# Three 256-column matmuls per weight block become one of 512 and one of 256 columns, with the PSUM halves added afterwards

## The chip, the cores and the metric

The kernel runs on one core of one Trainium2 chip. The metric is the device time of one execution in microseconds (us), as the median of several executions.

## What is computed

Two transformer layers are applied to one sequence of 256 tokens with a width of 2048, all in float32. The first layer mixes tokens with a causal multi-scale pooling and an RWKV-7 recurrence, then has a squared-ReLU feed-forward part and a gated embedding. The second mixes with gated linear attention (GLA) and a sparse attention (NSA), then has a SiLU-gated feed-forward part. The change touches only how some dense products are computed. Cut to those:

```python
z = rms_norm(x, attn_norm) @ w_in
h2 = rms_norm(x, mlp_norm)
x = x + jnp.square(jax.nn.relu(h2 @ w_ffn_up)) @ w_ffn_down
...
proj = n @ w_in_2
f = silu(m @ w_gate) * (m @ w_up)
x = x + f @ w_down
```

## The kernel before, in words

TensorE has a fast float32 mode (`F32R` in the code) that rounds its operands. To keep float32 accuracy the kernel splits each operand into a high part, rounded to that mode, and a low part, the remainder, and adds three products: high times high, high times low, low times high. The activations are split once, by `split` (lines 247 to 249): ScalarE copies the value to the rounded high part, VectorE subtracts it to get the low part. The weights are split as they arrive: `stream` (lines 236 to 245) takes a 128x1024 block of raw weights that a DMA has loaded, ScalarE writes its high part `h` (line 240), VectorE its low part `l` (line 244; in the first mixer one block in eight goes to GpSimd).

There are two kinds of dense product.

- `gemm_a` (lines 251 to 266) makes one output tile with 128 output features on the partitions and 256 tokens on the columns. A piece of the weight, 128x128, is the stationary operand and the activation, 128x256, is the moving one. A tile runs over 16 such pieces (two raw blocks of eight) with three matmuls each (lines 262 to 264), and all 48 add into the same 256 columns of PSUM. `first_tiles` (lines 363 to 376) does the same for three tiles at once at the start of each layer (lines 373 to 375).
- `gemm_b_part` (lines 729 to 744) has the activation as the stationary operand and 512 columns of weights as the moving one (lines 740 to 742). The change leaves it as it is.

`gemm_a` and `first_tiles` together make 216 tiles: 35 in the first layer's mixer (24 of them in `rwkv_front`, 8 in `pool_path`, 3 in `first_tiles`), 64 in its feed-forward part (`w_ffn_up`, line 838), 29 in the second mixer, and 88 in the second feed-forward part (`ffn2`, lines 1343 and 1346). With 16 pieces each that is 3456 pieces.

Results leave PSUM from the pool `acc`, four banks of 128x512. One VectorE multiplication by the row scale takes a tile out in most places (lines 352, 640, 922, 939, 1188, 1343, 1346); in the first feed-forward part it is a ReLU on ScalarE (line 840), and VectorE then squares the result (line 842). In `rwkv_front` and `pool_path` two tiles share one bank, 256 columns each (lines 423 to 425 and 633 to 635). Throughout the recurrence one of the four banks is held by `rwkv_post`.

The order of the instructions on each engine comes from a scheduler in the language's tile layer, which lays out the whole program by its own estimates; each engine then runs its queue in that order. A change of one instruction's length can therefore move others.

Of the kernel before, what the change touches and what calls it, by code (L numbers as in the profile page):

```python
# [19 lines left out]
T = 256  # L20
# [148 lines left out]
class Kern:  # L169
# [81 lines left out]
    def gemm_a(self, w, i, act, o=None):  # L251
        nc = self.nc
        if o is None:
            o = self.acc.tile([128, 512], F32, name="acc", tag="acc")[:, :T]
        n = len(act)
        k = 0
        for half in range(n // 8):
            h, l = self.stream(w[i, half].rearrange("p k n -> p (k n)"))
# [7 lines left out]
        return o  # L266

    def act_pair(self):
        return [self.big.tile([128, 16, T], F32R, name="x" + p, tag="x" + p) for p in "hl"]

    def act_tiles(self):
        return [[x[:, k] for k in range(16)] for x in self.act_pair()]

    def quart_tile(self, part, dtype=F32):
        return self.quart.tile([128, 4, T], dtype, name="q" + part, tag="q" + part)

    def half_tiles(self, parts=2):
        out = [], []
        for _ in range(parts):
            for side, part in zip(out, "hl"):  # L280
                q = self.quart_tile(part, F32R)
                side += [q[:, k] for k in range(4)]
        return out
# [18 lines left out]
    def block1_in(self):  # L302
        nc, I = self.nc, self.I
        xh, xl = self.act_tiles()
# [10 lines left out]
        for q in range(4):  # L315
            r = self.quart_tile("h")
            raws.append(r)
# [3 lines left out]
            for k in range(4):  # L321
                g = self.p("attn_norm", q * 4 + k)
                nc.scalar.activation(xh[q * 4 + k], r[:, k], AF.Copy, scale=g)
                nc.vector.scalar_tensor_tensor(xl[q * 4 + k], r[:, k], g, xh[q * 4 + k].bitcast(F32), ALU.mult, ALU.subtract)
        self.raws = raws
        return list(zip(xh, xl))

    def block1_stats(self):
# [3 lines left out]
        for q, r in enumerate(self.raws):  # L332
            sq = self.quart_tile("l")
# [13 lines left out]
    def shifted(self, pool, ps, mu, tag, out=None, bufs=2):  # L347
# [4 lines left out]
        nc.vector.tensor_mul(z[:, 1:], ps, self.rb)  # L352
# [10 lines left out]
    def first_tiles(self, w, n, act):  # L363
        nc = self.nc
        out = [self.acc.tile([128, 512], F32, name="acc", tag="acc")[:, :T] for _ in range(n)]
        for half in range(2):
            for i in range(n):
                h, l = self.stream(w[i, half].rearrange("p k n -> p (k n)"))
                for q in range(8):
                    k = half * 8 + q  # L370
                    wh, wl = h[:, q * 128:(q + 1) * 128], l[:, q * 128:(q + 1) * 128]
                    xh, xl = act[k]
                    nc.tensor.matmul(out[i], wh, xh, start=k == 0, stop=False)
                    nc.tensor.matmul(out[i], wh, xl, start=False, stop=False)
                    nc.tensor.matmul(out[i], wl, xh, start=False, stop=k == 15)  # L375
# [22 lines left out]
    def rwkv_front(self, j, act):  # L398
# [8 lines left out]
        if j in (3, 4):  # L407
            x = self.quart_tile("h").rearrange("p k t -> p (k t)")
            AR = x[:, :512].rearrange("p (c x t) -> p c x t", c=4, x=2)
            BKt = x[:, 512:].rearrange("p (c t) -> p c t", c=4)  # L410
            G = self.quart_tile("l").rearrange("p k t -> p (k t)").rearrange("p (h c t) -> p h c t", h=2, c=4)
# [4 lines left out]
        if j == 3:  # L416
            x = self.quart_tile("l").rearrange("p k t -> p (k t)")
# [962 lines left out]
```

## Time and profile before

| | us |
|---|---|
| median of 3 runs | 2485.6 (2485.5 to 2490.12) |
| profiled execution, first to last instruction (its span; the page gives no other time for it) | 2485.7 |
| TensorE matmul busy | 2455.0 (99%) |
| TensorE weight load busy | 2224.1 (89%) |
| VectorE busy | 1547.7 (62%) |
| ScalarE busy | 1149.9 (46%) |
| GpSimd busy | 217.5 (9%) |

In the profile PE is TensorE's matmuls, PEld its weight loads, DVE is VectorE, ACT is ScalarE, POOL is GpSimd. Matmuls are pipelined: a record lasts from a matmul's start until its last result is written, and the next starts long before that. So the busy time of PE only says whether there was a matmul under way; what a matmul costs is the distance from its start to the start of the next.

The stages, by the places of their lines in the trace: the first mixer until about 375 us, its output projection until about 450 us, the first feed-forward part until about 1150 us, the gated embedding until about 1297 us, the second mixer and its projection until about 1720 us, the second feed-forward part until the end.

### The profile page before, as it was taken

To read this page: it belongs to the slowest core of one execution; us is meant where nothing else is said; L and a number is where in the kernel's file an instruction comes from. 1 tells how busy PE (TensorE), PEld (TensorE's weight loads), DVE (VectorE), ACT (ScalarE), POOL (GpSimd) and SP (SyncE) were. 2 spreads that over 40 slices of the span, in tenths; PEclk is the share of its full clock that TensorE was granted. 3 is DMA by queue.
4 is the path that set the end of the run, shared out by engine and by line. 5 is a ranking of instruction groups with operands and counts; after the bars stand their busy time and mean duration, and the time that the engine had idled before them with its cause. 6 is when DMAs were issued, how large, how long until landed. Compare 5 with 4: busy or idle time off the path is not lost.

```text
span 2485.7 us, 40916 instructions
## 1 busy us (share of the span) xinstructions
PE 2455.0 (99%) x16396; PEld 2224.1 (89%) x16396; DVE 1547.7 (62%) x2436; ACT 1149.9 (46%) x1686; POOL 217.5 (9%) x321
## 2 busy tenths in 40 slices
PE   9999999999999999999999998999999999999999
PEld 8988888989989989988887897888989999998988
DVE  7788866555555555556674677766555555555555
ACT  5545445544444444445652466545444444444443
POOL 1543320000000000000010044200000000000000
PEclk9999999999999999999999999999999999999999
DMA  6443336555555555556556543255555655555554
GB/s 230 153 130 111 97 115 237 182 192 186 187 190 185 188 192 187 187 189 235 180 184 213 179 149 118 90 196 185 179 190 185 187 186 186 188 185 187 186 190 158
DMA packets 135406, 439.59 MB, mean 177 GB/s; under 512 B 26784, under 2 KB 29216, under 8 KB 134064
## 3 DMA queue, kind: packets, MB, share of 16 engines
q1 hardware_dynamic: 130032, 423.58, 52.1%
q10 hardware_dynamic: 5184, 13.41, 1.4%
q8 instruction: 128, 2.10, 0.3%
q14 instruction: 62, 0.51, 0.1%
HBM read 429.59 MB, written 7.34 MB: 176 GB/s over the span
## 4 chain that ended last, share of the span: by engine, by line
PE 94%; DVE 4%; ACT 1%; DMA 1%; issue 1%; POOL 0%; SPq 0%; DVEq 0%; ACTq 0%
PE acc L262 16%; PE acc L263 16%; PE acc L264 16%; PE acc L740 13%; PE acc L741 13%; PE acc L742 13%; PE ch L361 3%; PE fr L361 2%; DVE l L244 1%; PE fr L782 1%; PE acc L361 1%; PE ch L582 0%; PE ch L585 0%; DVE X L1002 0%; PE acc L375 0%
## 5 line engine op out<-in xcount | busy, mean ns | idle before, releaser
L244 DVE TENSOR_TENSOR l<-r,h 128x1024 fp32r<-128x1024 f32 x774 | 951.5, 1230 | 737.0 <-ACT h L240 728.8
L240 ACT CAST h<-r 128x1024 fp32r<-128x1024 f32 x780 | 818.8, 1050 | 1102.2 <-PE acc L742 448.1
L262 PE MATMUL acc<-qh,h 128*128 128x256 f32 x1824 | 520.8, 286 | 0.0
L264 PE MATMUL acc<-qh,l 128*128 128x256 f32 x1824 | 519.3, 285 | 0.0
L263 PE MATMUL acc<-ql,h 128*128 128x256 f32 x1824 | 519.2, 285 | 0.0
L264 PE MATMUL acc<-xh,l 128*128 128x256 f32 x1536 | 439.0, 286 | 0.5 <-DVE l L244 0.5
L262 PE MATMUL acc<-xh,h 128*128 128x256 f32 x1536 | 439.4, 286 | 0.0
L263 PE MATMUL acc<-xl,h 128*128 128x256 f32 x1536 | 438.6, 286 | 0.0
L262 PEld LDWEIGHTS acc<-qh,h 128*128 128x128 f32 x1824 | 350.5, 192 | 4.0 <-issue 3.5
L263 PEld LDWEIGHTS acc<-ql,h 128*128 128x128 f32 x1824 | 350.5, 192 | 1.7 <-issue 1.2
L264 PEld LDWEIGHTS acc<-qh,l 128*128 128x128 f32 x1824 | 350.2, 192 | 1.1 <-issue 0.9
L741 PE MATMUL acc<-l,qh 128*128 128x512 f32 x768 | 300.4, 391 | 0.0
L742 PE MATMUL acc<-h,ql 128*128 128x512 f32 x768 | 299.3, 390 | 0.0
L263 PEld LDWEIGHTS acc<-xl,h 128*128 128x128 f32 x1536 | 295.8, 193 | 2.7 <-issue 1.3
L262 PEld LDWEIGHTS acc<-xh,h 128*128 128x128 f32 x1536 | 295.6, 193 | 2.8 <-issue 0.9
L264 PEld LDWEIGHTS acc<-xh,l 128*128 128x128 f32 x1536 | 295.7, 193 | 2.5 <-DVE l L244 0.7
L740 PE MATMUL acc<-h,qh 128*128 128x512 f32 x768 | 275.2, 392 | 0.0
L741 PE MATMUL acc<-l,xh 128*128 128x512 f32 x608 | 237.2, 390 | 0.0
L742 PE MATMUL acc<-h,xl 128*128 128x512 f32 x608 | 236.3, 389 | 0.0
L740 PE MATMUL acc<-h,xh 128*128 128x512 f32 x608 | 214.7, 390 | 0.0
L740 PEld LDWEIGHTS acc<-h,qh 128*128 128x128 f32 x768 | 144.0, 188 | 30.8 <-issue 1.2
L741 PEld LDWEIGHTS acc<-l,qh 128*128 128x128 f32 x768 | 144.2, 188 | 29.9 <-issue 0.4
(413 smaller groups left out, 2418.4 us busy)
## 6 DMA issues: line engine op xcount, KB each, us to landing
r<-w_ffn_up SPq DMA_DIRECT2D x128, 512.0 KB, 3.3
r<-w_ffn_down SPq DMA_DIRECT2D x128, 512.0 KB, 3.4
r<-w_gate SPq DMA_DIRECT2D x88, 512.0 KB, 3.9
r<-w_up SPq DMA_DIRECT2D x88, 512.0 KB, 3.5
r<-w_down SPq DMA_DIRECT2D x88, 512.0 KB, 4.2
r<-w_in SPq DMA_DIRECT2D x70, 512.0 KB, 3.4
r<-w_out SPq DMA_DIRECT2D x64, 512.0 KB, 3.3
r<-w_in_2a SPq DMA_DIRECT2D x58, 512.0 KB, 3.3
```

The lines of the kernel that those rows point to most:

```text
L240: nc.scalar.copy(h, r)
L244: eng.tensor_sub(l, r, h.bitcast(F32))
L262: nc.tensor.matmul(o, wh, xh, start=k == 0, stop=False)
L263: nc.tensor.matmul(o, wh, xl, start=False, stop=False)
L264: nc.tensor.matmul(o, wl, xh, start=False, stop=k == n - 1)
L361: self.nc.tensor.matmul(out, lhsT, rhs, start=start, stop=stop)
L740: nc.tensor.matmul(ps[t], ah, wh, start=first and k == 0, stop=False)
L741: nc.tensor.matmul(ps[t], ah, wl, start=False, stop=False)
L742: nc.tensor.matmul(ps[t], al, wh, start=False, stop=last and k == nk - 1)
L782: nc.tensor.transpose(ps[:, o:o + 128], self.x[:, t, kk * 128:kk * 128 + 128], self.c("ident"))
```

## The change

The high and the low part of an activation are now laid side by side in one tile (`xs` and `qs` in place of `xh`/`xl` and `qh`/`ql`), so that one access pattern of two pieces of 256 columns reads both. A piece of the weight then needs two matmuls: its high part times both activation parts, 512 columns, into a whole PSUM bank; and its low part times the activation's high part, 256 columns, into the bank's upper half. The lower half holds high times high, the upper half the two small products, and the new helper `join` adds them: ScalarE copies the upper half to a tile `low`, VectorE adds the lower half to it, and VectorE multiplies by the row scale where there is one. Every tile now fills a bank, so the pairs in `rwkv_front` and `pool_path` take two banks. The tile `low` shares its buffer with others: in the first mixer with `d` of `shifted` (tag `zd`, one buffer), in the second with the tanh tiles (tag `cth`, two).

In the first feed-forward part `join` takes the place of the ReLU on ScalarE, and the squaring becomes one VectorE instruction that takes the maximum with zero and multiplies.

```diff
-    def gemm_a(self, w, i, act, o=None):
-        nc = self.nc
-        if o is None:
-            o = self.acc.tile([128, 512], F32, name="acc", tag="acc")[:, :T]
-        n = len(act)
-        k = 0
-        for half in range(n // 8):
+    def gemm_a(self, w, i, act):
+        o = self.acc.tile([128, 512], F32, name="acc", tag="acc")
+        for half in range(len(act) // 8):
             h, l = self.stream(w[i, half].rearrange("p k n -> p (k n)"))
-            for q in range(8):
-                wh, wl = h[:, q * 128:(q + 1) * 128], l[:, q * 128:(q + 1) * 128]
-                xh, xl = act[k]
-                nc.tensor.matmul(o, wh, xh, start=k == 0, stop=False)
-                nc.tensor.matmul(o, wh, xl, start=False, stop=False)
-                nc.tensor.matmul(o, wl, xh, start=False, stop=k == n - 1)
-                k += 1
+            self.block_mms(o, h, l, act[half * 8:half * 8 + 8], half == 0, half == len(act) // 8 - 1)
         return o
 
+    def block_mms(self, o, h, l, act, first, last):
+        mm = self.nc.tensor.matmul
+        for q, x in enumerate(act):
+            wh, wl = h[:, q * 128:(q + 1) * 128], l[:, q * 128:(q + 1) * 128]
+            mm(o.rearrange("p (a t) -> p a t", a=2), wh, x, start=first and q == 0, stop=False, skip_group_check=True)
+            mm(o[:, T:], wl, x[:, 0], start=False, stop=last and q == len(act) - 1, skip_group_check=True)
+
+    def join(self, out, ps, scale=None):
+        nc = self.nc
+        pool, tag, bufs = self.low
+        low = pool.tile([128, T], F32, name="low", tag=tag, bufs=bufs)
+        nc.scalar.copy(low, ps[:, T:])
+        nc.vector.tensor_add(out, ps[:, :T], low)
+        if scale is not None:
+            nc.vector.tensor_mul(out, out, scale)
+
     def act_pair(self):
-        return [self.big.tile([128, 16, T], F32R, name="x" + p, tag="x" + p) for p in "hl"]
+        return self.big.tile([128, 2, 16, T], F32R, name="xs", tag="xs")
...
-        nc.vector.tensor_mul(z[:, 1:], ps, self.rb)
+        self.join(z[:, 1:], ps, self.rb)
         d = F.tile([128, T], F32, name="d", tag="zd")
...
-        rk = self.acc.tile([128, 512], F32, name="acc", tag="acc")
-        for q in range(2):
-            self.gemm_a(w, 3 + 3 * j + q, act, rk[:, q * T:q * T + T])
-        zr = self.shifted(F, rk[:, :T], self.p("mu_rkv", j), "r", bufs=1)
-        zk = self.shifted(F, rk[:, T:], self.p("mu_rkv", 8 + j), "k", bufs=1)
+        rk = [self.gemm_a(w, 3 + 3 * j + q, act) for q in range(2)]
+        zr = self.shifted(F, rk[0], self.p("mu_rkv", j), "r", bufs=1)
+        zk = self.shifted(F, rk[1], self.p("mu_rkv", 8 + j), "k", bufs=1)
...
                 ps = self.gemm_a(I["w_ffn_up"], s * 8 + i, act)
                 a = tp.tile([128, T], F32, name="relu", tag="relu")
-                nc.scalar.activation(a, ps, AF.Relu)
+                self.join(a, ps)
                 b = tp.tile([128, T], F32, name="relu2", tag="relu2")
-                nc.vector.tensor_mul(b, a, a)
-                self.split(hh[i], hl[i], b)
+                nc.vector.scalar_tensor_tensor(b, a, 0.0, a, ALU.max, ALU.mult)
+                self.split(hidden[i][:, 0], hidden[i][:, 1], b)
...
-                nc.vector.tensor_mul(g, self.gemm_a(I["w_gate_2"], j, act), rb)
+                self.join(g, self.gemm_a(I["w_gate_2"], j, act), rb)
                 nc.scalar.activation(g, g, AF.Silu)
                 u = tp.tile([128, T], F32, name="u", tag="u")
-                nc.vector.tensor_mul(u, self.gemm_a(I["w_up_2"], j, act), rb)
+                self.join(u, self.gemm_a(I["w_up_2"], j, act), rb)
```

`first_tiles` calls `block_mms` too, and `pool_path`, `scaled`, `conv` and the compression inputs of the second mixer read their tiles through `join` in the same way.

In the order of the instructions the change shows at three places. The first is TensorE in the first mixer, where the sums for the first head normalisation (`sq`) and the first small matmul on `z` stand among the matmuls of `gemm_a`. Before:

```order
L262 MATMUL acc<-xh,h 128x256
L263 MATMUL acc<-xl,h 128x256
L264 MATMUL acc<-xh,l 128x256
L262 MATMUL acc<-xh,h 128x256
L263 MATMUL acc<-xl,h 128x256
L361 MATMUL fr<-cst,sq 128x2 x2
L361 MATMUL fr<-z,lora 128x256
```

Now:

```order
L262 MATMUL acc<-xs,h 128x512
L263 MATMUL acc<-xs,l 128x256
L262 MATMUL acc<-xs,h 128x512
L369 MATMUL fr<-cst,sq 128x2 x2
L369 MATMUL fr<-z,lora 128x256
```

Three rows for each piece of the weight have become two. The same two small products come 45 pieces after the row scale of the tokens (`rs`) before, and 78 pieces after it now.

The second place is VectorE in the first mixer, where the first tiles of the recurrence leave PSUM between the subtractions `l<-r,h` that split the weights. Before:

```order
L389 TENSOR_SCALAR z<-z 128x256 x2
L352 TENSOR_TENSOR z<-acc,rb 128x256 x2
L244 TENSOR_TENSOR l<-r,h 128x1024
L357 SCALAR_TENSOR_TENSOR z<-d,cols,z 128x256 x2
L244 TENSOR_TENSOR l<-r,h 128x1024
L352 TENSOR_TENSOR z<-acc,rb 128x256
```

Now:

```order
L391 TENSOR_SCALAR z<-z 128x256
L270 TENSOR_TENSOR z<-acc,low 128x256
L272 TENSOR_TENSOR z<-z,rb 128x256
L365 SCALAR_TENSOR_TENSOR z<-d,cols,z 128x256
L270 TENSOR_TENSOR z<-acc,low 128x256
L272 TENSOR_TENSOR z<-z,rb 128x256
L244 TENSOR_TENSOR l<-r,h 128x1024
L365 SCALAR_TENSOR_TENSOR z<-d,cols,z 128x256
```

Two tiles left together before (x2); now each goes through an addition, a multiplication and the token shift (`z<-d,cols,z`) before the next begins.

The third is VectorE in the first feed-forward part, for one tile of the hidden layer. Before:

```order
L244 TENSOR_TENSOR l<-r,h 128x1024
L842 TENSOR_TENSOR relu_5985<-relu 128x256
L244 TENSOR_TENSOR l<-r,h 128x1024
L249 TENSOR_TENSOR ql<-relu_5985,qh 128x256
L244 TENSOR_TENSOR l<-r,h 128x1024
```

Now:

```order
L244 TENSOR_TENSOR l<-r,h 128x1024
L270 TENSOR_TENSOR relu<-acc,low 128x256
L841 SCALAR_TENSOR_TENSOR relu_5511<-relu 128x256
L244 TENSOR_TENSOR l<-r,h 128x1024
L249 TENSOR_TENSOR qs<-relu_5511,qs 128x256
```

The addition is new on VectorE; the two weight subtractions for each tile stand where they were.

## Rows read from the trace of the kernel before

**Rows 1.** The page: busy time and share of each engine; the chain that ended last.

```profile
PE 2455.0 (99%) x16396; PEld 2224.1 (89%) x16396; DVE 1547.7 (62%) x2436; ACT 1149.9 (46%) x1686; POOL 217.5 (9%) x321
...
PE 94%; DVE 4%; ACT 1%; DMA 1%; issue 1%; POOL 0%; SPq 0%; DVEq 0%; ACTq 0%
```

**Rows 2.** Stretches: from:to, length, then busy PE, PEld, DVE, ACT, POOL, granted clock, DMA.

```profile
0.00:50.00 50.00, 45.14 (x295) 39.16 (x296) 38.90 (x66) 26.53 (x38) 6.35 (x20) 0.97 0.68 248
100.00:200.00 100.00, 94.17 (x760) 87.56 (x760) 84.21 (x229) 47.36 (x89) 44.60 (x66) 0.95 0.41 122
1300.00:1350.00 50.00, 44.30 (x266) 35.52 (x266) 26.36 (x29) 11.74 (x13) 6.41 (x4) 0.93 0.61 214
1500.00:1600.00 100.00, 91.83 (x647) 82.15 (x647) 81.35 (x165) 59.39 (x114) 37.36 (x40) 0.93 0.31 101
400.00:1150.00 750.00, 750.00 (x4771) 684.61 (x4771) 420.68 (x491) 330.28 (x429) 1.31 (x1) 1.00 0.58 190
1700.00:2450.00 750.00, 750.00 (x5270) 706.73 (x5269) 424.41 (x502) 314.35 (x368) 0.00 (x0) 1.00 0.58 186
```

**Rows 3.** Timeline of TensorE, `gemm_a`: start, length, engine, line, out<-in, shape.

```profile
599.78 0.28 PE L262 MATMUL acc<-xh,h 128*128 128x256 f32 x1
599.90 0.28 PE L263 MATMUL acc<-xl,h 128*128 128x256 f32 x1
600.02 0.28 PE L264 MATMUL acc<-xh,l 128*128 128x256 f32 x1
...
603.50 0.28 PE L263 MATMUL acc<-xl,h 128*128 128x256 f32 x1
```

**Rows 4.** Timeline of TensorE in `gemm_b_part`.

```profile
900.04 0.39 PE L742 MATMUL acc<-h,ql 128*128 128x512 f32 x1
900.26 0.39 PE L740 MATMUL acc<-h,qh 128*128 128x512 f32 x1
...
905.93 0.39 PE L741 MATMUL acc<-l,qh 128*128 128x512 f32 x1
```

**Rows 5.** Groups by form: count, busy us, mean ns, idle before and its end.

```profile
L262 PE MATMUL acc<-qh,h 128*128 128x256 f32 x1824 | 520.8, 286 | 0.0
L262 PE MATMUL acc<-xh,h 128*128 128x256 f32 x1536 | 439.4, 286 | 0.0
L375 PE MATMUL acc<-xh,l 128*128 128x256 f32 x48 | 14.5, 305 | 3.4 <-DVE l L244 3.4
L373 PE MATMUL acc<-qh,h 128*128 128x256 f32 x48 | 13.6, 286 | 0.0
```

**Rows 6.** Timelines of TensorE: a moving operand of two pieces (KT), one of one piece (z).

```profile
1455.75 0.60 PE L361 MATMUL ch<-KT,QT 128*128 128x256 f32 x2
...
243.20 1.02 PE L361 MATMUL acc<-z,lorag 128*128 128x256 f32 x4
```

**Rows 7.** Groups by form: what reads PSUM or splits weights on VectorE and ScalarE.

```profile
L244 DVE TENSOR_TENSOR l<-r,h 128x1024 fp32r<-128x1024 f32 x774 | 951.5, 1230 | 737.0 <-ACT h L240 728.8 <-PE fr L361 0.5
L240 ACT CAST h<-r 128x1024 fp32r<-128x1024 f32 x780 | 818.8, 1050 | 1102.2 <-PE acc L742 448.1 <-PE acc L263 347.6 <-issue 261.6
L842 DVE TENSOR_TENSOR relu<-relu 128x256 f32<-128x256 f32 x64 | 26.7, 418 | 0.0
L840 ACT ACTIVATE relu<-acc 128x256 f32<-128x256 f32 x64 | 24.2, 379 | 0.0
L352 DVE TENSOR_TENSOR z<-acc,rb 128x256 f32<-128x256 f32 x27 | 10.5, 419 | 5.1 <-PE acc L264 4.9
L357 DVE SCALAR_TENSOR_TENSOR z<-d,cols,z 128x256 f32<-128x256 f32 x19 | 9.1, 480 | 4.0 <-POOL d L354 3.9
```

**Rows 8.** What TensorE waited for, longest first: us in total, times, longest.

```profile
PE ch L361 <- DVE X L1002: 5.7, 1, 5.7
PE acc L375 <- DVE l L244: 3.4, 3, 1.8
PE ch L545 <- DVE x L539: 3.3, 1, 3.3
```

More of the change, by code (lines that the diff above doesn't have):

```diff
@@ L268, in act_pair, with quart_tile @@
     def act_pair(self):
-        return [self.big.tile([128, 16, T], F32R, name="x" + p, tag="x" + p) for p in "hl"]
+        return self.big.tile([128, 2, 16, T], F32R, name="xs", tag="xs")
     def act_tiles(self):
-        return [[x[:, k] for k in range(16)] for x in self.act_pair()]
-    def quart_tile(self, part, dtype=F32):
-        return self.quart.tile([128, 4, T], dtype, name="q" + part, tag="q" + part)
+        x = self.act_pair()
+        return [x[:, :, k] for k in range(16)]
+    def quart_tile(self, dtype=F32):
+        return self.quart.tile([128, 2, 4, T], dtype, name="qs", tag="qs")
@@ L277, in half_tiles @@
     def half_tiles(self, parts=2):
-        out = [], []
+        out = []
         for _ in range(parts):
-            for side, part in zip(out, "hl"):
-                q = self.quart_tile(part, F32R)
-                side += [q[:, k] for k in range(4)]
+            q = self.quart_tile(F32R)
+            out += [q[:, :, k] for k in range(4)]
         return out
@@ L331, in block1_stats @@
         parts = []
-        for q, r in enumerate(self.raws):
-            sq = self.quart_tile("l")
+        for q, both in enumerate(self.raws):
+            r, sq = both[:, 0], both[:, 1]
             nc.scalar.activation(sq, r, AF.Square)
@@ L364, in first_tiles @@
         nc = self.nc
-        out = [self.acc.tile([128, 512], F32, name="acc", tag="acc")[:, :T] for _ in range(n)]
+        out = [self.acc.tile([128, 512], F32, name="acc", tag="acc") for _ in range(n)]
         for half in range(2):
@@ L368, in first_tiles @@
                 h, l = self.stream(w[i, half].rearrange("p k n -> p (k n)"))
[L369 to L375, printed above, removed]
+                self.block_mms(out[i], h, l, act[half * 8:half * 8 + 8], half == 0, half == 1)
         return out
@@ L632, in pool_path @@
             ds = []
-            ps2 = self.acc.tile([128, 512], F32, name="acc", tag="acc")
+            ps2 = [self.gemm_a(self.I["w_in"], 27 + 2 * g + q, act) for q in range(2)]
             for q in range(2):
-                self.gemm_a(self.I["w_in"], 27 + 2 * g + q, act, ps2[:, q * T:q * T + T])
-            for q in range(2):
-                ps = ps2[:, q * T:q * T + T]
                 u = U.tile([128, 64 + T], F32, name="u", tag="vp", bufs=2)[:, :16 + T]
                 nc.gpsimd.memset(u[:, :16], 0.0)
-                nc.vector.tensor_mul(u[:, 16:], ps, self.rb)
+                self.join(u[:, 16:], ps2[q], self.rb)
                 a, m = u, 1
@@ L679, in block1_mix @@
         self.fp = self.pool("fp", 1, es=es)
+        self.low = self.fp, "zd", 1
         act = self.block1_in()
@@ L700, in block1_mix @@
         self.rwkv_inverse(tiles[6:])
-        for side, more in zip(mixr, self.half_tiles(1)):
-            side += more
+        mixr += self.half_tiles(1)
         self.rwkv_post(tiles[4:6], mixr, bank)
@@ L749, in out_proj @@
     def out_proj(self, w, first, second, k_first, finish):
-        halves = [list(zip(*m)) for m in (first, second)]
+        halves = [first, second]
         k0 = (0, 8) if k_first == 0 else (8, 0)
@@ L767, in begin_norm @@
         parts = [self.half_tiles(), self.half_tiles()] if halves else [self.act_tiles()]
-        self.n_act = [x for part in parts for x in zip(*part)]
+        self.n_act = [x for part in parts for x in part]
         self.n_ss = self.small.tile([128, 2, 4], F32, name="nss", tag="nss", bufs=2)
@@ L913, in block2 @@
         self.sh = self.pool("sh", 1)
+        self.low = self.sh, "cth", 2
         self.gp = self.pool("gla", 1)
@@ L1334, in ffn2 @@
         tp = self.pool("ffn2", 2, es=es)
+        self.low = tp, "low", 2
         act = self.n_act
-        hidden = self.act_tiles()
+        tiles = self.act_tiles()
         for s in range(6):
             nh = 8 if s < 5 else 4
-            hh, hl = (x[s % 2 * 8:s % 2 * 8 + nh] for x in hidden)
+            hidden = tiles[s % 2 * 8:s % 2 * 8 + nh]
             for i in range(nh):
```

54 lines of the change are left out of this document (29 added, 25 removed).

## Prediction

> **What bounds the kernel now.** I read the page first, then the busy times of a few stretches, then TensorE's timeline, then the groups and the waits. The page says that TensorE had a matmul under way for 99% of the span and that 94% of the chain that ended last is TensorE [rows 1]. The stretches say where this is strict: in both feed-forward parts it is busy for all of 750 us, at the full granted clock (1.00, 2.4 GHz), while VectorE works 421 and 424 us of the 750 and ScalarE 330 and 314. In the mixers it is not: TensorE idles 5.8 us in the 100 us from 100 and 8.2 us in the 100 us from 1500, and VectorE is 84% and 81% busy there [rows 2]. So the feed-forward parts go at the pace at which matmuls start, and the mixers nearly so, with VectorE close behind.
>
> The pace stands in the timeline. In `gemm_a` 31 matmuls start between 599.78 and 603.50: 0.1200 us each for 256 columns [rows 3]. In `gemm_b_part` 26 start between 900.04 and 905.93: 0.2265 us each for 512 columns [rows 4]. The 0.28 and 0.39 us in the same rows are lengths of pipelined records and not prices. Doubling the columns adds 0.1065 us, so a column costs 0.416 ns, which is one cycle at 2.4 GHz, and both lengths carry the same remainder of 0.0135 us per matmul. Both streams bring a new stationary operand with each matmul, in the same fast mode, so the remainder belongs to a matmul with its weight load, whatever its length.
>
> **What the change does, part by part.** *Matmuls.* A piece of the weight cost 3 x 0.1200 = 0.3600 us and now costs 0.2265 + 0.1200 = 0.3465: the columns stay 768, one matmul and its load go, and 0.0135 us with them. The groups give the count: 1536 + 1824 pieces in `gemm_a` and 48 + 48 in `first_tiles`, 3456 in all [rows 5]. 3456 x 0.0135 = **46.7 us off TensorE**. Of the pieces, 48 in the opening run while TensorE waits for the first low parts (3.4 us before line 375 in that group [rows 5]); I count their 0.6 us as not gained.
>
> *The new access pattern.* The moving operand of the 512-column matmul has two pieces, 16 KB or 4 KB apart. I looked for such a read in the old kernel. The scores of the sparse attention (line 1135) read KT in two pieces of 128 for the first token block; two such matmuls take 0.60 us, and four of the same size from one piece take 1.02 us. A record alone lasts about 0.38, so a start costs 0.22 and 0.21 us [rows 6]. A gap in the read is thus free to within what rows of two decimals can show. I take 0.2265; the bad end is that the second piece pays the 0.0135 again and nothing is gained.
>
> *The rule on the other side.* The remainder is 0.0135 us at both lengths [rows 3, 4]. The Trainium skill, page "TensorE: Matmul & The Clock Gate", section "Back-to-back issue gap", gives a gap of columns over 2.4 GHz plus about 2.5 ns, and this case's trace does not agree: by it 256 and 512 columns would take 109 and 216 ns, against 120 and 226.5 measured. By the page 3456 removed starts would be worth an estimated 8.6 us and the sum would end near 2477. The measurement decides.
>
> *Leaving PSUM.* Each of 216 tiles gets a ScalarE copy of 256 columns, for which I take the ReLU from PSUM, 0.379 us, and a VectorE addition, for which I take the multiplication from PSUM, 0.419 us; 0.80 us together [rows 7]. In the first feed-forward part the copy replaces the ReLU, and the square goes from 0.418 to 0.480 us (the price of line 357, which has the same form) [rows 7]. There VectorE gets 64 x (0.42 + 0.06) = 31 us, on 421 of 750 us; in the second part 88 x 0.42 = 37 us, on 424, and ScalarE 88 x 0.38 = 33 us, on 314 [rows 2]. Both stay under two thirds busy, so TensorE covers them. What could still be late is the weight split: ScalarE's 1.05 us and VectorE's 1.23 us for a block [rows 7], while eight pieces will take 2.77 us. An exit that goes first delays a split by 0.8 us, and three buffers of split weights hold that. I charge nothing there; without this cover the same work would cost 0.80 us a tile.
>
> *In the mixers* the cover is thin. 35 + 29 = 64 tiles gain 0.80 us each, 51 us. How much shows? VectorE's share of the last chain is 4% of the span, 99 us [rows 1]; outside the two full stretches VectorE was busy 1547.7 - 420.7 - 424.4 = 703 us [rows 1, 2], so some 14% of its work there is on the chain. 14% of 51 is **7.2 us given back**. The ends are none of it and half of it (25.6 us). Half would be right if the token shift sets the end: `low` and `d` share one buffer, so the three tiles of a recurrence step leave one after another, as the order shows, with GpSimd's subtraction between, and behind them wait the head sums, the recurrence and, in VectorE's queue, the next weight splits. An end below zero exists as well: the scheduler has laid the mixers out anew, and TensorE idles 24.6 us in the four loose stretches [rows 2]; a quarter of that back is 6 us.
>
> *PSUM banks.* r and k fill a bank each now. With one bank held for the output there are three for r, k and v, so r's bank is wanted again after k and v, 2 x 16 x 0.3465 = 11.1 us later. The exit needs 0.80 us and at most a few splits of 1.05 and 1.23 us ahead of it [rows 7], and the longest waits of TensorE name no exit from such a bank [rows 8]. No charge.
>
> **Sum.** 46.7 - 0.6 - 7.2 = 38.9 us. The profiled execution's span is 2485.7 us, 0.1 above the median of the three runs, so no correction is needed: 2485.7 - 38.9 = 2446.8, say **2447 us**.
>
> **Rivals.** (1) *The mixers become VectorE's.* Over half of the 51 us shows, and TensorE's pauses cost clock besides: where it idles today the mean granted clock is 0.93 to 0.95 [rows 2], and 0.05 over 100 us is 5 us of matmul time. For it speak VectorE's 84%, against it that the added VectorE work of the first mixer, 35 x 0.42 = 14.7 us over some 350 us, is 4 points. With 25.6 us and up to 10 more for the clock it ends between 2465 and 2475.
>
> (2) *The start is not given back in full*, because the alternation of 512 and 256 columns or the second piece of the read pays for it. With a fifth of the gain left (0.2 x 46.7 = 9.3 us) and the mixers covered the time is about 2476. With nothing left and 7.2 us given back it is 2493, with the mixers covered 2486. Against it stand equal remainders at two lengths and the read of KT [rows 3, 4, 6]. The page's rule named above would put the time near the first of these.
>
> (3) *Slower: the ring of PSUM banks runs dry.* If TensorE stood at a tile's start until an older tile has left, each tile would cost up to 0.80 us: 216 x 0.80 = 173 us, less 46.7, so 2612. The point from which it decides is 46.7 / 216 = 0.22 us of standing per tile. Its place would be the recurrence, where a bank is refilled after two tiles. If only the 24 tiles there stood, 2.3 us each (a copy and an addition behind a split of each engine, 3.1 us, less what overlaps) would make 55 us and the kernel 8 us slower, 2494. Against it: 11.1 us until the refill.
>
> (4) *The change does not do what it says.* The order shows two matmuls where there were three, and 512 columns in the first, so this is left with (2).
>
> **How the numbers follow.** Forecast 0.74, (1) 0.14, (2) 0.08, half of it at about 2476 and half at no change or slightly above, (3) 0.04. A measurement of this kernel can tell about 0.2%, 5 us, from no change. Faster: 0.74 + 0.14 + 0.04 = 0.92; the same: 0.04; slower: 0.04. The range goes from the full 46.7 us with 6 us of idle time regained, 2433, to the upper bound of the mixers' charge, 2485.7 - 46.1 + 25.6 = 2465; what lies above is rivals 1 to 3 in the main.
>
> **What would show it.** In the changed profile the feed-forward parts should still have TensorE busy throughout; the 512-column matmul should start its successor after 0.2265 us, the 256-column one after 0.120, and a tile of 16 pieces should take 5.54 us in place of 5.76. The first feed-forward part should be 64 x 16 x 0.0135 = 13.8 us shorter, the second 88 x 16 x 0.0135 = 19.0. The mixers should be shorter by 64 x 16 x 0.0135 = 13.8 less about 8. A pair of starts of 0.36 us would prove the first step wrong; waits of TensorE on the addition or the copy out of `acc`, the last one; mixers that are longer than before, the share of 14%.

## The result and the profile after

The changed kernel takes 2506.51 us (median of 4 runs, 2502.6 to 2512.53) against 2487.86 us for the kernel before on the same chip. The ratio is 1.0074 with a 95% interval of 1.0055 to 1.0092: **slower by 0.7%**, where 1.6% faster was forecast.

The page of the changed kernel has these two lines for [rows 1], the busy time of each engine and the chain that ended last:

```profile
PE 2443.6 (98%) x12940; PEld 2041.4 (81%) x12940; DVE 1635.4 (65%) x2652; ACT 1188.4 (47%) x1838; POOL 223.7 (9%) x321
...
PE 88%; DVE 7%; ACT 2%; issue 1%; DMA 1%; POOL 1%; SPq 0%; DVEq 0%; ACTq 0%; POOLq 0%
```

TensorE starts 3456 matmuls fewer and is busy for only 11.4 us less; its share of the last chain fell from 94% to 88%, VectorE's rose from 4% to 7%. To see where that happened I cut the span at marks that both programs have: the end of the first mixer with its projection (`r2`), the end of the first feed-forward part (`rh`), the scaling of the tokens that ends the embedding, and the first and last SiLU of the second feed-forward part. The stretches of the kernel before, in the columns of [rows 2]:

```profile
0.00:476.71 476.71, 464.03 (x3392) 408.46 (x3393) 358.62 (x829) 237.19 (x432) 135.70 (x232) 0.99 0.48 156
476.71:1196.66 719.95, 719.95 (x4613) 658.47 (x4612) 406.60 (x477) 318.07 (x415) 0.00 (x0) 1.00 0.58 191
1294.82:1747.78 452.96, 439.09 (x2720) 381.02 (x2719) 302.29 (x559) 235.74 (x403) 81.83 (x89) 0.98 0.49 161
1747.78:2454.96 707.18, 707.18 (x5041) 669.68 (x5040) 398.86 (x461) 292.55 (x337) 0.00 (x0) 1.00 0.58 186
```

and the same four of the changed kernel:

```profile
0.00:499.29 499.29, 471.61 (x2814) 379.40 (x2815) 378.36 (x863) 245.63 (x467) 139.28 (x232) 0.97 0.46 149
499.29:1211.84 712.55, 712.55 (x3606) 604.10 (x3605) 433.63 (x540) 317.29 (x415) 0.00 (x0) 1.00 0.58 193
1308.56:1780.14 471.58, 442.01 (x2280) 361.43 (x2279) 315.12 (x591) 247.04 (x434) 84.45 (x89) 0.97 0.46 157
1780.14:2476.85 696.71, 696.71 (x3682) 596.23 (x3681) 427.74 (x546) 313.93 (x423) 0.00 (x0) 1.00 0.57 189
```

The account: first mixer +22.6 us, first feed-forward part -7.4, embedding -1.4, second mixer +18.6, second feed-forward part -10.5, tail -2.2: +19.7 together, the difference between the two spans. The feed-forward parts gained half of what was forecast, and the mixers turned a forecast gain of 6 us (13.8 less 7.2 and 0.6) into a loss of 41.2. In the feed-forward parts TensorE is busy for the whole stretch still. In the mixers it idles 27.7 and 29.6 us instead of 12.7 and 13.9, which is 30.7 us of the 41.2; the other 10.5 are longer busy time (471.61 and 442.01 us against 464.03 and 439.09), although some 1000 matmuls fell away there. The mean granted clock fell from 0.99 and 0.98 to 0.97: in the trace's clock records TensorE is at 1.2 GHz for 54.6 us of the two mixers, against 34.1 before.

The pace, as in [rows 3], from TensorE's timeline of the changed kernel in `gemm_a` of the first feed-forward part:

```profile
599.86 0.40 PE L262 MATMUL acc<-xs,h 128*128 128x512 f32 x1
600.09 0.28 PE L263 MATMUL acc<-xs,l 128*128 128x256 f32 x1
600.21 0.40 PE L262 MATMUL acc<-xs,h 128*128 128x512 f32 x1
600.45 0.28 PE L263 MATMUL acc<-xs,l 128*128 128x256 f32 x1
...
603.39 0.40 PE L262 MATMUL acc<-xs,h 128*128 128x512 f32 x1
```

Ten pairs start between 599.86 and 603.39: 0.353 us each, where 0.3465 was forecast and three matmuls took 0.3600. Averaged over the starts of both feed-forward parts, the successor of a 512-column matmul follows after 0.2358 us and that of a 256-column one after 0.1166. So the pair is some 7.5 ns shorter, not 13.5.

That is an average of two rhythms. In the same program 207 pairs on end, from 1782.1 to 1853.9 us, start 0.3467 us apart, which is the price forecast; ten of them:

```profile
1805.00 0.40 PE L262 MATMUL acc<-qs,h 128*128 128x512 f32 x1
1805.23 0.28 PE L263 MATMUL acc<-qs,l 128*128 128x256 f32 x1
1805.35 0.39 PE L262 MATMUL acc<-qs,h 128*128 128x512 f32 x1
...
1808.47 0.40 PE L262 MATMUL acc<-qs,h 128*128 128x512 f32 x1
```

So do 79 pairs from 509.5 us. The long stretches that come straight from `gemm_b_part`, 128 or 256 pieces each, take 0.3532 or 0.3533 a pair from end to end, and every run with this form in its feed-forward parts has the same two kinds at the same places. In the changed kernel both fast stretches stand behind a place where the queue has two 512-column matmuls in a row and, some eight pieces later, two of 256. No run looked for what sets the rhythm.

What TensorE waited for, longest first, answers [rows 8]:

```profile
PE acc L263 <- DVE l L244: 9.8, 6, 2.5
PE fr L369 <- DVE m L1140: 8.2, 1, 8.2
PE acc L1205 <- DVE cc L1198: 7.9, 2, 4.2
PE acc L262 <- DVE z L270: 4.2, 2, 2.3
PE fr L369 <- DVE hx L224: 3.1, 1, 3.1
PE acc L262 <- DVE sp L270: 2.8, 1, 2.8
PE ch L369 <- ACT G L554: 2.5, 2, 2.0
PE acc L262 <- DVE cc L270: 2.0, 1, 2.0
```

No single wait is large. The longest row is the low part of a weight block that comes late from VectorE (`l`), 9.8 us where `gemm_a` and `first_tiles` together waited 3.9 before. The additions of `join` (line 270) hold banks that `gemm_a` wants, for 9.0 us in all; the rest is mostly steps of the dependent chains that come late (`m` and `cc` in the second mixer, `hx` and `G` in the first). The groups of the exit itself, with the columns of [rows 7]:

```profile
L269 ACT COPY low<-acc 128x256 f32<-128x256 f32 x216 | 78.8, 365 | 48.4 <-DVE z L365 25.6 <-DVE vp L365 16.5 <-PE acc L263 4.9
L270 DVE TENSOR_TENSOR z<-acc,low 128x256 f32<-128x256 f32 x27 | 11.3, 420 | 1.5 <-ACT low L269 1.3
L272 DVE TENSOR_TENSOR z<-z,rb 128x256 f32<-128x256 f32 x27 | 16.5, 612 | 0.4
L365 DVE SCALAR_TENSOR_TENSOR z<-d,cols,z 128x256 f32<-128x256 f32 x19 | 12.3, 648 | 7.4 <-POOL d L362 7.3
L841 DVE SCALAR_TENSOR_TENSOR relu<-relu 128x256 f32<-128x256 f32 x64 | 27.1, 425 | 2.1
```

The prices of the added work were right: 0.365 and 0.420 us where 0.379 and 0.419 were taken, and the square cost 0.425, not 0.480. Two steps that were there before became dearer: the row scale of `z` takes 0.612 us instead of 0.419, and the token shift 0.648 instead of 0.480 [rows 7]. And the copy stood for 42.1 us (25.6 + 16.5) behind `z` and `vp` of line 365: those read `d`, which has the buffer that `low` wants next.

### The profile page after: what moved, and what is told of

The parts are those of the page before. It is cut to its first block, busy times and chain, and to the rows that moved or that the text cites. A ratio compares the mean times of both kernels' runs of the same rounds, so it can differ in the third digit from the quotient of the medians.

```text
span 2505.4 us, 34364 instructions
## 1 busy us (share of the span) xinstructions
PE 2443.6 (98%) x12940; PEld 2041.4 (81%) x12940; DVE 1635.4 (65%) x2652; ACT 1188.4 (47%) x1838; POOL 223.7 (9%) x321
## 4 chain that ended last, share of the span: by engine, by line
PE 88%; DVE 7%; ACT 2%; issue 1%; DMA 1%; POOL 1%; SPq 0%; DVEq 0%; ACTq 0%; POOLq 0%
PE acc L262 29%; PE acc L263 15%; PE acc L738 13%; PE acc L739 13%; PE acc L740 13%; PE ch L369 2%; DVE l L244 2%; PE fr L369 1%; DVE xt L525 1%; ACT h L240 1%; PE fr L780 1%; DVE X L527 0%; PE acc L369 0%; PE ch L583 0%; DVE xs L332 0%
## 5 line engine op out<-in xcount | busy, mean ns | idle before, releaser
L262 PE MATMUL acc<-qs,h 128*128 128x512 f32 x1872 | 670.9, 402 | 4.8 <-DVE sp L270 2.8
L262 PE MATMUL acc<-xs,h 128*128 128x512 f32 x1584 | 572.0, 404 | 4.2 <-DVE z L270 4.2
L263 PE MATMUL acc<-qs,l 128*128 128x256 f32 x1872 | 532.1, 285 | 5.0 <-DVE l L244 5.0
L263 PE MATMUL acc<-xs,l 128*128 128x256 f32 x1584 | 451.0, 285 | 4.8 <-DVE l L244 4.8
L262 PEld LDWEIGHTS acc<-qs,h 128*128 128x128 f32 x1872 | 355.0, 190 | 92.7 <-issue 5.6
L263 PEld LDWEIGHTS acc<-qs,l 128*128 128x128 f32 x1872 | 357.2, 191 | 8.7 <-DVE l L244 5.6
L263 PEld LDWEIGHTS acc<-xs,l 128*128 128x128 f32 x1584 | 303.0, 191 | 10.4 <-DVE l L244 6.5
L739 PE MATMUL acc<-l,qs 128*128 128x512 f32 x768 | 301.0, 392 | 0.0
L740 PE MATMUL acc<-h,qs 128*128 128x512 f32 x768 | 299.3, 391 | 0.0
L738 PE MATMUL acc<-h,qs 128*128 128x512 f32 x768 | 278.7, 395 | 1.4 <-ACT qs L248 1.4
L740 PE MATMUL acc<-h,xs 128*128 128x512 f32 x608 | 236.2, 389 | 0.0
L738 PE MATMUL acc<-h,xs 128*128 128x512 f32 x608 | 215.2, 390 | 0.2 <-DVE x_res L810 0.2
```

The costliest lines, as they stand in the source:

```text
L262: mm(o.rearrange("p (a t) -> p a t", a=2), wh, x, start=first and q == 0, stop=False, skip_group_check=True)
L263: mm(o[:, T:], wl, x[:, 0], start=False, stop=last and q == len(act) - 1, skip_group_check=True)
L738: nc.tensor.matmul(ps[t], ah, wh, start=first and k == 0, stop=False)
L739: nc.tensor.matmul(ps[t], ah, wl, start=False, stop=False)
L740: nc.tensor.matmul(ps[t], al, wh, start=False, stop=last and k == nk - 1)
```

## The experiments

Stage lengths below are in the order first mixer with projection, first feed-forward part, second mixer, second feed-forward part: before 476.7, 720.0, 453.0, 707.2; changed 499.3, 712.6, 471.6, 696.7. They come from one profiled execution each; medians and ratios come from the timed runs. For the two mixers together I compare sums: 929.7 before, 970.9 changed.

**e1: high and low part side by side.** The moving operand becomes one piece of 512 columns.

```diff
-        return self.big.tile([128, 2, 16, T], F32R, name="xs", tag="xs")
+        return self.big.tile([128, 16, 2, T], F32R, name="xs", tag="xs")
```

> The changed kernel with the high and low part of each 256-token piece laid next to each other, so that the 512-column matmul reads one piece of 512 columns instead of two of 256. Theory A (the gap in the read is what makes the 512-column matmul 0.235 us instead of 0.2265): its successor starts after 0.2265 us, the first feed-forward part falls from 712.6 to about 704 us and the second from 696.7 to about 685 us, the whole by 20 to 29 us to about 2480. Rival B (the alternation of 512 and 256 columns costs it, or two matmuls on one set of weights): the pair stays at 0.353 us and the time at about 2506.

Measured: ratio 1.0067 (1.005 to 1.0084), stages 500.3, 712.5, 473.7, 696.7, starts 0.2358 and 0.1166 us. The read in two pieces costs nothing; the forecast's step on the access pattern stands.

**e2: `low` gets its own buffer in the first mixer** (a buffer of `lorag` pays for the space).

```diff
-        self.low = self.fp, "zd", 1
+        self.low = self.fp, "low", 1
```

> The changed kernel with a buffer of its own for low in the first mixer (one, paid for with one of the two buffers of a weight of the output gate). Theory C (ScalarE stands at the copy until the token shift has read d out of the shared buffer, and the weight splits behind it in ScalarE's queue come late): ScalarE's waits at the copy for line 365, 42 us now, go, and the first mixer with its projection falls from 499 us by 10 to 20 us; the second mixer stays at 471.6. Rival D (the additional exits themselves, or the new order, cost the mixer): the waits go but the first mixer stays within 5 us of 499.

Measured: ratio 1.0036 (1.0023 to 1.0049), first mixer 492.0, second, which this edit leaves alone, 470.7. The shared buffer costs 7.3 us of the 22.6, less than theory C's 10 to 20 and more than rival D allowed. The copy still stands in line, now for its own last reader. What ScalarE waited for in the first mixer, of the changed kernel and then of e2:

```profile
ACT low L269 <- DVE z L365: 25.6, 12, 6.5
ACT low L269 <- DVE vp L365: 16.5, 7, 3.7
```

```profile
ACT low L269 <- DVE z L270: 25.5, 8, 4.9
```

**e3: the old form in the mixers, the new one in the feed-forward parts.** The mixers call the three matmuls and the single exit of the old kernel.

```diff
+        if self.low is None:
+            return self.gemm_three(w, i, act, o)
...
-        self.low = self.fp, "zd", 1
+        self.low = None
```

> Both mixers with three 256-column matmuls per piece, one exit per tile and shared banks as in the kernel before; the feed-forward parts as in the changed kernel. Theory E (all of the loss arises in the mixers through the exits): first mixer with projection 476.7 us, second 453 us, feed-forward parts 712.6 and 696.7, the whole about 2468. Rival F (the new layout of the activations or the scheduler's new arrangement costs the mixers without the exits): the mixers stay over 490 and 465 us and the whole over 2490.

Measured: 2469.14 us, ratio 0.9926 (0.9911 to 0.994), stages 475.7, 712.5, 454.2, 696.7. The loss sits wholly in the mixers, and the feed-forward parts keep their gain.

**e4: the new exit with three matmuls of 256 columns.** High times high goes to the lower half of the bank, the small products to the upper half, and `join` adds them.

```diff
-            mm(o.rearrange("p (a t) -> p a t", a=2), wh, x, start=first and q == 0, stop=False, skip_group_check=True)
+            mm(o[:, :T], wh, x[:, 0], start=first and q == 0, stop=False, skip_group_check=True)
+            mm(o[:, T:], wh, x[:, 1], start=False, stop=False, skip_group_check=True)
```

> Three 256-column matmuls per piece everywhere, the first into the lower and the two others into the upper half of the bank, and the exits of the changed kernel: the exits alone without the longer matmul. Theory E: the feed-forward parts stand at 720 and 707 us as before, both mixers are as long as in the changed kernel or up to 8 us longer, the whole 2525 to 2535. Rival G (the mixers were lengthened by the mixed matmuls, not by the exits): the mixers are back at 477 and 453 us and the whole at 2486.

Measured: ratio 1.0062 (1.0045 to 1.0079), stages 491.6, 720.0, 457.1, 709.8. Both theories missed: the exits, with the order that the scheduler gives them, lengthen the mixers by 14.9 and 4.1 us, less than the whole change and more than nothing. In the feed-forward parts they are covered, but for 2.6 us in the second.

**e5: the feed-forward form of e3, sorted by length.** Eight 512-column matmuls of a block, then its eight of 256.

```diff
         for q, x in enumerate(act):
             wh, wl = h[:, q * 128:(q + 1) * 128], l[:, q * 128:(q + 1) * 128]
             mm(o.rearrange("p (a t) -> p a t", a=2), wh, x, start=first and q == 0, stop=False, skip_group_check=True)
+        for q, x in enumerate(act):
+            wl = l[:, q * 128:(q + 1) * 128]
             mm(o[:, T:], wl, x[:, 0], start=False, stop=last and q == len(act) - 1, skip_group_check=True)
```

> As the run with the change in the feed-forward parts alone, but with the eight 512-column matmuls of a block first and its eight 256-column ones behind them. Theory H (each change of length between neighbouring matmuls costs, some 0.006 us for a pair): inside a block the starts are 0.2265 and 0.120 us apart, the pair 0.3465; the feed-forward parts fall from 712.5 to about 706 us and from 696.7 to about 688 us, the whole from 2469 to about 2454. Rival I (a 512-column matmul of this kind costs 0.235 us wherever it stands): 512 columns stay at 0.235, the 256-column ones go back to 0.120, and the time is 2469 to 2475.

Measured: **2457.67 us, ratio 0.9881 (0.9866 to 0.9895)**, the fastest kernel of the study; feed-forward parts 707.4 and 692.4. Its timeline of TensorE where a `gemm_b_part` (line 767) gives way to `gemm_a`; successive matmuls of a line stand in one row:

```profile
645.09 0.39 PE L767 MATMUL acc<-h,qs 128*128 128x512 f32 x1
645.32 1.98 PE L281 MATMUL acc<-xs,h 128*128 128x512 f32 x8
647.13 1.11 PE L284 MATMUL acc<-xs,l 128*128 128x256 f32 x8
648.08 2.00 PE L281 MATMUL acc<-xs,h 128*128 128x512 f32 x8
649.92 1.11 PE L284 MATMUL acc<-xs,l 128*128 128x256 f32 x8
650.88 1.32 PE L281 MATMUL acc<-xs,h 128*128 128x512 f32 x5
```

The first eight of 512 columns follow others of 512 and take 647.13 - 645.32 = 1.81 us, 0.226 each: the forecast's price. The next eight follow matmuls of 256 and take 1.84. So in this order it is the change of length that costs. Averaged over the groups that follow 256 columns, the eight 512-column matmuls take 233, 236, 228, 233, 231, 227, 227 and 227 ns from start to start (227 all along in the 12 that follow 512), those of 256 after a change 113, 119 and then 120. A change there and back costs some 20 ns net (28 more for the eight of 512, 8 less for those of 256), once for every eight pieces here. In the changed kernel it comes with every piece and costs 9 - 3 = 6 ns on average, but nearly nothing in the stretches at 0.3467: a change of length alone doesn't settle the price.

**e6: the third product goes to the bank's lower half** (with the mixers of e3), a single run.

```diff
-            mm(o[:, T:], wl, x[:, 0], start=False, stop=last and q == len(act) - 1, skip_group_check=True)
+            mm(o[:, :T], wl, x[:, 0], start=False, stop=last and q == len(act) - 1, skip_group_check=True)
```

> As the run with the change in the feed-forward parts alone, but the third product is added into the lower half of the bank instead of the upper, which the 512-column matmul wrote last. Theory J (the successor of the 512-column matmul waits because it adds to the columns that were written last): 512 columns go from 0.235 to about 0.2265 us and the feed-forward parts to about 706 and 688 us. Rivals H and I: 0.235 and 0.117 us as they are, 712.5 and 696.7 us.

Measured: 2470.42 us, starts 0.2358 and 0.1166. Which half the third product adds to makes no difference.

**e7: the changed matmuls and banks without the added exit in the mixers.**

```diff
+        if self.low is None:
+            nc.vector.tensor_mul(out, ps[:, :T], scale)
+            return
...
-        self.low = self.fp, "zd", 1
+        self.low = None
```

> The changed kernel, but in both mixers only the lower half of a bank is read, with the one multiplication of the kernel before: the copy and the addition are left out there, so the two small products do not reach the result. Matmuls, banks and layouts are those of the changed kernel. Theory E (the exits make the loss): the first mixer with projection falls from 499 to about 473 us and the second from 471.6 to about 450, the whole to about 2460. Rival K (banks of their own for r and k, or the mixed matmuls in the mixers, make it): they stay over 490 and over 465, the whole over 2490.

Measured: ratio 0.998 (0.997 to 0.9989), mixers 483.3 and 462.4. Without the copy and the addition they are 25.2 us shorter than changed, but still 16.0 longer than before, with fewer matmuls and the old exit. Something beside the exits lengthens them.

**e8: the old kernel with r, k and the pool pairs in banks of their own.**

```diff
-        rk = self.acc.tile([128, 512], F32, name="acc", tag="acc")
-        for q in range(2):
-            self.gemm_a(w, 3 + 3 * j + q, act, rk[:, q * T:q * T + T])
+        rk = [self.gemm_a(w, 3 + 3 * j + q, act) for q in range(2)]
```

> The kernel before with one thing changed: r and k, and the two tiles of a pooling group, each get a bank of their own, read by the same single multiplication. Theory E: no change, 476.7 us for the first mixer with projection within 4, the whole within 0.2% of before. Rival K (three banks are too few for r, k and v): the first mixer grows by 8 to 20 us, and TensorE is seen waiting for a read of a bank.

Measured: ratio 0.9999 (0.9989 to 1.0008), mixers 475.4 and 452.7. The banks cost nothing.

What is left in e7 is the order. I counted the weight pieces that stand ahead of a few marks in TensorE's queue:

```
                                      e8    e7   changed
first sums of a head norm (sq)        99   102   134
first row sums of Y                  413   466   472
third row sums of Y                  494   542   541
last use of E in the GLA            1955  1986  1986
```

With the changed matmuls the scheduler puts up to 59 more pieces ahead of the steps of the dependent chains, and in e7 up to 53.

**e9 and e10: TensorE's order of e8, pinned** in the mixers of the changed kernel (e9) and of e7 (e10). Each matmul or piece gets an order-only dependency on the one that is ahead of it in e8's queue; ScalarE, VectorE and GpSimd keep the scheduler's freedom.

```diff
+        for a, b in zip(order, order[1:]):
+            tc.add_manual_dep(log[b][0], log[a][-1].name, mybir.DependencyInfo(
+                mybir.DependencyClass.NoSync, mybir.DependencyReason.DATA), reason="order")
```

> The changed kernel, with TensorE's order in both mixers pinned to the order that the old program (with r, k and the pool pairs in banks of their own) had: each small product stands behind the same number of weight pieces as there. Nothing else is pinned and nothing is left out. Theory O (the scheduler's new order lengthens the mixers by about the 6.6 and 9.4 us that the kernel without the added exits keeps, and by what the cheaper pieces should have given): the first mixer with its projection takes 484 to 492 us instead of 499.3, the second 455 to 463 instead of 471.6, and the kernel 2482 to 2494. Theory X (the added exits delay the chains, whatever the order; an order made for another program makes it worse): 499 and 472 or more, 2506 or more.

> The kernel with the changed matmuls that leaves out the copy and the addition in the mixers (only the bank's lower half is read there, so the two small products are left out of the mixers' results), with TensorE's order in the mixers pinned to that of the old program. Theory O (order): with the same order as the old program and pieces that are 0.0075 us cheaper the mixers cost no more than before: 470 to 477 us for the first with its projection (before 476.7, unpinned 483.3) and 448 to 454 for the second (before 453.0, unpinned 462.4); the kernel 2457 to 2468. Theory M (the mixed matmuls themselves stretch the mixers, by their clock or by the weight splits that must come earlier): 481 to 485 and 460 to 464 as without the pin, 2478 to 2484.

Measured: e10 2464.67 us, ratio 0.9902 (0.9887 to 0.9916), mixers 473.9 and 453.4; e9 2515.0 us, ratio 1.0107 (1.009 to 1.0124), mixers 497.1 and 477.0. The mixers' stretches of e7:

```profile
0.00:483.28 483.28, 466.28 (x2814) 377.32 (x2815) 360.01 (x828) 236.92 (x432) 136.65 (x232) 0.97 0.48 154
1292.54:1754.91 462.37, 440.85 (x2280) 361.06 (x2279) 305.02 (x562) 239.26 (x405) 81.65 (x89) 0.97 0.48 160
```

and of e10:

```profile
0.00:473.92 473.92, 457.10 (x2814) 371.09 (x2815) 361.37 (x829) 237.67 (x432) 135.29 (x232) 0.99 0.49 157
1284.35:1737.73 453.38, 438.94 (x2274) 358.77 (x2273) 303.77 (x562) 237.70 (x406) 85.86 (x89) 0.98 0.49 162
```

The two programs have the same instructions and differ in their order alone. The old order gives back 18.4 us, the mean clock with it. So in e7 it is the order, and nothing in the matmuls. The way differs between the mixers. In the first TensorE idles as long in e7 as in e10 (17.0 and 16.8 us) but is busy for 9.2 us longer, with the clock at 1.2 GHz for 27.3 us against 10.2. In the second the idle time makes most of it, 21.5 us against 14.4. With the exits in, e9 fails its theory of the order: the pinned order helps the first mixer by 2.2 us and costs the second 5.4. There the chains come so late that the places of the old order don't fit. The longest waits of TensorE in e9 (its lines are numbered differently: 208 are small matmuls, 211 transposes):

```profile
PE acc L211 <- DVE cc L1264: 18.6, 5, 5.4
PE fr L208 <- ACT sq L500: 14.6, 4, 7.1
PE ch L208 <- DVE X L1068: 14.2, 1, 14.2
```

TensorE stands for results that have gone through an exit and a few steps more, `cc` behind `conv`'s exit and `sq` behind those of the recurrence. At a pinned order the exits cost 974.1 - 927.3 = 46.8 us, nearly the whole 51 us of their work.

**e11: e5 with the two parts side by side** (the edits of e1 and e5 together).

> Old mixers, new feed-forward parts with the eight 512-column matmuls of a block first and the eight of 256 behind, and now the high and low part of an activation side by side, so that the moving operand is one piece of 512. If the read in two pieces is what keeps successive 512-column matmuls at 0.2304 us instead of 0.2268: 0.2268, the first feed-forward part 3.5 us shorter than with the two-piece read (707.4), the second 4.8 (692.4), the kernel about 2449. If the read is free and the rest belongs to something else: 0.2304 again, 707 and 692, 2457 to 2458.

Measured: 2461.21 us, ratio 0.9895 (0.9877 to 0.9913), feed-forward parts 707.4 and 692.4 as in e5. The read in two pieces is free in the sorted order too.

**e12: the exit without ScalarE.** One VectorE sum over both halves, straight from PSUM.

```diff
-        low = pool.tile([128, T], F32, name="low", tag=tag, bufs=bufs)
-        nc.scalar.copy(low, ps[:, T:])
-        nc.vector.tensor_add(out, ps[:, :T], low)
+        nc.vector.reduce_sum(out, ps.rearrange("p (a t) -> p t a", a=2), AX.X)
```

> The changed kernel with another exit everywhere: in place of ScalarE's copy of the upper half and VectorE's addition one VectorE sum over the two halves, straight from PSUM (512 elements in, 256 out; sums of 512 elements take 0.68 us elsewhere in the kernel), and the multiplication as before. Nothing is left out. Theory H (the hand-over through ScalarE makes the exits long: its copy stands for the shared buffer and behind weight splits, 42 us of standing in the first mixer): the first mixer with its projection takes 480 to 490 us in place of 499.3, the second 458 to 465 in place of 471.6, the kernel 2482 to 2497. Theory V (VectorE's added time in the chains costs, by whatever road): VectorE gets 0.68 instead of 0.42 per tile, so 499 and 472 or more, 2506 to 2515. The feed-forward parts stay at 712.6 and 696.7 in both.

Measured: 2491.9 us, ratio 1.0016 (1.0006 to 1.0026), stages 485.7, 712.6, 463.4, 696.9. The new instruction in the first mixer:

```profile
L267 DVE TENSOR_REDUCE z<-acc 128x256 f32<-128x512 f32 x27 | 18.5, 686 | 0.7 <-PE acc L263 0.6
```

VectorE works 0.686 us per tile in place of 0.420, and the mixers are 21.8 us shorter. So it was not VectorE's time that cost but the road through two engines. The run doesn't part what belongs to that road: with the copy go its shared buffer and ScalarE's work, and the scheduler lays the mixers out anew (111 pieces ahead of the first head sums, 134 in the changed kernel).

## Why the prediction was wrong

*Matmuls, 46.7 us: mis-sized.* The remainder of 0.0135 us per start is right for a stream of one length (0.2265 and 0.1200, and 1.81 us for eight in e5). The step that failed is the sentence that the remainder belongs to a matmul with its weight load "whatever its length": it was read from two streams that never change length and used for one that changes at every start. There it holds in some stretches (0.3467 a pair) and not in most (0.3532). On average a removed start brought some 0.0075 us, so the 2432 pieces of the feed-forward parts gave 7.4 + 10.5 = 17.9 us instead of 32.8. Rival 2 named the alternation and had 0.08, with a fifth of the gain left where over half was. What sets the rhythm is open.

The figure that the forecast weighed against its own, some 2.5 ns a start (the Trainium skill, page "TensorE: Matmul & The Clock Gate", section "Back-to-back issue gap"; the section gives it for an isolated matmul, not for a stream with weight loads), would have given 2432 x 0.0025 = 6 us there. The measurement lies between the two, and in sorted order (12.5 + 14.8 = 27.3 us) near the forecast. The forecast's 2477 for that figure is the time with nothing given back in the mixers; with its own 7.2 us the sum would be 2484.

*The read in two pieces, no charge:* right (e1, e11), though not by its ground: the matmuls on KT and `z` in [rows 6] cost 0.21 us for 256 columns where those of `gemm_a` cost 0.12, so they couldn't show a gap in the read at that pace. *PSUM banks, no charge:* right for the banks themselves (e8); that no exit would be waited for was not, with 9.0 us in the changed kernel.

*The exits in the feed-forward parts, no charge:* right. TensorE is busy throughout; only e4 shows 2.6 us in the second part.

*The mixers, 7.2 us given back: the step that decided.* They became 41.2 us longer. "14% of its work there is on the chain" priced a delay by a share of busy time. VectorE's busy share in the first mixer hardly moved (358.62 of 476.71 is 75.2%, 378.36 of 499.29 is 75.8%), so rival 1's VectorE as the bound isn't what happened. What grew is the time from the last matmul of a tile to the next small matmul of its chain. For the first head, from the last matmul of k's tile to the head sums, before:

```profile
45.97 0.28 PE L264 MATMUL acc<-xh,l 128*128 128x256 f32 x1
53.53 0.50 PE L361 MATMUL fr<-cst,sq 128*128 128x2 f32 x4
```

and in the changed kernel:

```profile
43.69 0.28 PE L263 MATMUL acc<-xs,l 128*128 128x256 f32 x1
62.77 0.50 PE L369 MATMUL fr<-cst,sq 128*128 128x2 f32 x4
```

That is 7.6 and 19.1 us; it is 7.7 in e7 without the added exit, 11.1 in e12 and 13.9 in e2. The runs split the 41.2 us in steps, each a difference of two sums of the mixers:

| step | sum of the mixers | step's part |
|---|---|---|
| before | 929.7 | |
| changed matmuls, old order and exit (e10) | 927.3 | -2.4 |
| the scheduler's new order (e7) | 945.7 | +18.4 |
| halves added by one VectorE instruction (e12) | 949.1 | +3.4 |
| by ScalarE and VectorE (changed) | 970.9 | +21.8 |

The parts depend on the path: exits and order answer each other, as e9 shows, and e4 has the exits with three matmuls at 19.0 us. On any path the exit through two engines is dear. The shared buffer, which the forecast named for its upper end and did not charge, is 7.3 us of it (e2). The order was mentioned too, as a possible gain of 6 us; it was a loss. Part of the new order's 18.4 us is clock, which rival 1 had named: in the mixers of e7 it is 0.97, in those of e10 0.99 and 0.98, as before. It doesn't simply follow the idle time, which in the first mixer is the same in both, and no run took it apart from the rest.

*Rival 3, slower,* had the sign and a time of 2494, but another mechanism: the banks are not what ran dry.

Open: why the scheduler puts more pieces ahead of the chains in e7, where a piece became only 2% cheaper; its estimates were not looked into. The 1.4 and 2.2 us gained in the embedding and the tail were not followed either; the second belongs to neither mixers nor matmuls, since it came with every kernel that has the copy in its exit (28.3 to 29.2 us) and not with e12 (30.8).

## What to carry to other kernels

A price read from a uniform stream holds for uniform streams: before costing a mixed one, look for a place in the trace where the length changes, and if there is none, sort by length. An average over starts can hide two rhythms, so look at the starts one by one. An added step between PSUM and a dependent chain is priced by its latency, every queue it stands in included, not by its engine's busy share; one longer instruction on one engine beat two short ones on two (e12), and work with slack is where such a step is free (e3, e5). Where a scheduler lays out the program, pin the old order once: it tells the cost of the change from the cost of the new layout.

## What the runs showed of the hardware

- In groups of eight (e5) a matmul that follows one of another length starts its successor at another distance: 256 to 512 columns 233 ns, back at 227 with the sixth start; 512 to 256 columns 113 ns, back at 120 with the third.
- Strict alternation of 512 and 256 columns runs in two rhythms, 0.3467 or 0.3532 us a pair, each kept for up to 207 and 256 pairs on end; on average over the feed-forward parts the starts are 0.2358 and 0.1166 us apart.
- These averages are the same for a moving operand of one piece and of two (e1), and for either half of the bank (e6).
- VectorE multiplies by the row scale in 0.612 us where `z` is already in SBUF (line 272), 27 times, and in 0.425 for `u` (52 times); the same multiplication of `z` from PSUM took 0.419 before [rows 7]. No run looked for the reason.
